# Differential attention's weights: Z0 moved out of the split, low halves subtracted on GpSimd, and four maxima sent through DRAM

## Chip, core and metric

One core of a Trainium2 chip runs the whole program. The metric is the device time of one execution in microseconds (us). TensorE (PE in the rows) does the matrix products, VectorE (DVE), ScalarE (ACT) and GpSimd (POOL) work on tiles of 128 partitions, and SyncE (SP) issues every DMA. Each engine works through its own list of instructions in order and waits at an instruction until what it needs is there.

## The reference, cut to what matters

One encoder layer for two groups of requests with the same weights: `p` (2048 positions) and `s` (512). An input projection gives eight units of heads: four for dilated window attention (mixer A, units 0 to 3) and four for differential attention (mixer B, units 4 to 7). This change is in mixer B:

```python
def diff_attention(q, k, v, lam, g_sub, lam_init):
    def block(qblk):                                   # 128 queries
        sc = jnp.einsum('bqhmd,bkhmd->bhmqk', qblk, k).astype(jnp.float32) * scale
        p = jax.nn.softmax(sc, axis=-1)
        a = p[:, :, 0] - lam * p[:, :, 1]
        return jnp.einsum('bhqk,bkhe->bqhe', a.astype(v.dtype), v)
    ...
    return rmsnorm(o, g_sub) * (1.0 - lam_init)
```

So two softmax maps over all keys are subtracted, the difference multiplies V, and each row of the product is divided by its root mean square. A factor common to a row of `a` cancels in that norm, but for the epsilon. The mixers' outputs then go through one output projection, a second norm and a gated residual.

## The kernel before

All inputs are float32. Each matrix product is made of float16 pairs: a value is scaled by a power of two, rounded to float16 (the high half), and the rest is rounded again (the low half); three products, high by high, high by low and low by high, are added. The scale of a weight block comes from its largest magnitude, which `allmax` finds over all partitions: TensorE transposes the column of 128 maxima (L178), VectorE takes the maximum of the row (L180), and a second matmul spreads it (L182).

The program goes through the units in the order 4, 0, 5, 1, 6, 2, 7, 3, so stages of mixer B and of mixer A alternate, B first. In each stage it goes through five blocks of 512 positions, four of `p` and one of `s`. While a unit's attention runs, the projections of its next block and of the next unit are woven in (`interleave`, with costs that set the pace), so that TensorE has work between the pieces of attention. The weight block two units ahead is loaded, scaled (`raw_scale`) and split (`raw_split`) in the same stages. A scheduler then lays down each engine's list from the order in which the code is written, priorities, and a timeline that it simulates.

A block of mixer B has four items of 128 queries (`ItemB`), 16 in `p` and 4 in `s` for each of the four units. For an item of `p`, per softmax map m (0 and 1) and half of the keys: TensorE makes 128 by 1024 scores in PSUM (L602, L608); VectorE scales them and keeps the row's minimum of the negated scores (L611); ScalarE takes the exponential into a tile of the pool `pp` and sums it into Z (L618). Then VectorE forms `a = p1 * (-lam * Z0 / Z1) + p0` (L634, two halves), ScalarE writes the high half, `a` times `rz[:, 3:4]`, that is sigc / Z0 (L636), VectorE the low half (L644, in `tail1`), and each of these is transposed by a DMA into `at`, two per item of high halves and two of low. An item later, `tail2` has TensorE multiply the transposed weights by V (L656, 48 matmuls into one PSUM tile of the pool `pv`), ScalarE squares and sums the result (L663) and copies it (L664), GpSimd works out the norm's factor in three small steps (L666, L668, L669). `tail3` scales the rows (ScalarE, L675), transposes them on TensorE (L677, again a tile of `pv`), and VectorE multiplies by the gate (L681). An item of `s` has one half of 512 keys for each map. In the stages of mixer B, `pv` has a single buffer: the product of one item, its transposition and the next item's product follow each other through it. The scores have three buffers (`sc`).

GpSimd also does the rotary embedding of Q and K (L443 to L446), whose results ScalarE copies on (L547, L488). `y_out` writes a finished block of 512 positions to DRAM and keeps its maximum; when all eight units have written a block, the output projection (`out_proj`, L918) can take it, after `y_scale` has worked out its scale.

## Time and profile before

| | us |
|---|---|
| median of 3 runs (2176.42 to 2187.44) | 2182.41 |
| the profiled execution's own time | 2191.28 |
| its span, first to last instruction | 2189.5 |
| TensorE busy | 1910.8 |
| VectorE busy | 1541.1 |
| ScalarE busy | 1152.7 |
| GpSimd busy | 394.9 |

The profiled execution took 8.9 us more than the median of the runs. Its granted TensorE clock is 0.942 of full speed on average. Busy time is an average over unlike stages, so it is read by stage below; TensorE's busy time counts matmuls that overlap, so a busy TensorE is not yet one at its peak.

### The profile page before, as it was taken

Reading aid. Unit: us, or ns where it says so; the run is one execution under the profiler, and the core shown is the slowest. Engines: PE = TensorE matmul, PEld = TensorE weight load, DVE = VectorE, ACT = ScalarE, POOL = GpSimd, SP = SyncE. Lnnn points to the kernel's source line nnn. Section 1 sums busy time; section 2 is a strip of 40 time slices with the busy share of each in tenths; the row PEclk is TensorE's granted clock in tenths of the full one; section 3 lists DMA queues with packets and bytes.
Section 4 is the critical chain, followed back from the end, with each engine's and each line's share of the span. In section 5 each row is a group of like instructions: output and inputs, shape, how many; then the busy total and the mean of one; then the engine's idle time right before and its main releaser. Section 6 shows DMA issues by size and latency. Waiting matters only on the chain. (4 is left out here: it accounts for less than half of the span.)

```text
span 2189.5 us, 47689 instructions
## 1 busy us (share of the span) xinstructions
PE 1910.8 (87%) x18545; PEld 1285.2 (59%) x18545; DVE 1541.1 (70%) x3428; ACT 1152.7 (53%) x2278; POOL 394.9 (18%) x1049
## 2 busy tenths in 40 slices
PE   4878997898989988888899888897989878989898
PEld 2665665666767666666566666574665554444443
DVE  3777998676669988666599886666888665455543
ACT  3555665555547666555467665554566644333321
POOL 0122222221112222111122221111222121100000
PEclk7789999999999999999999999898999888999999
DMA  7585787888857789898477888888776779665553
GB/s 293 171 253 126 138 163 149 188 158 165 186 130 152 145 196 188 140 173 192 114 151 145 184 188 155 170 183 235 147 148 157 159 163 191 122 133 126 130 163 111
DMA packets 726834, 360.12 MB, mean 164 GB/s; under 512 B 639808, under 2 KB 686672, under 8 KB 723152
## 3 DMA queue, kind: packets, MB, share of 16 engines
q1 hardware_dynamic: 726608, 357.08, 73.6%
q8 instruction: 145, 2.38, 0.5%
q14 instruction: 81, 0.66, 0.1%
HBM read 164.79 MB, written 36.97 MB: 92 GB/s over the span
## 5 line engine op out<-in xcount | busy, mean ns | idle before, releaser
L460 PE MATMUL pj<-w,h 128*128 128x256 f16 x3840 | 480.9, 281 | 29.1 <-DVE V L476 8.2
L460 PEld LDWEIGHTS <-h 128*128 128x128 f16 x3840 | 379.1, 101 | 103.9 <-issue 40.5
L618 ACT ACTIVATE pp<-sc,nb 128x1024 f32<-128x1024 f32 (+1 forms) x288 | 304.3, 1060 | 100.2 <-DVE sc L611 83.2
L534 PE MATMUL pj<-w,h 128*128 128x128 f16 x3840 | 257.1, 223 | 15.0 <-ACT q L541 8.5
L534 PEld LDWEIGHTS <-h 128*128 128x128 f16 x3840 | 231.6, 100 | 43.4 <-issue 32.5
L557 PE MATMUL pj<-h,w 128*128 128x512 f16 x960 | 230.7, 392 | 17.9 <-ACT q L541 17.9
L656 PE MATMUL pv<-V,at 128*128 128x128 f16 x3072 | 207.5, 227 | 38.1 <-DVE yt L681 29.0
L656 PEld LDWEIGHTS <-at 128*128 128x128 f16 x3264 | 201.9, 102 | 64.6 <-issue 47.8
L747 DVE SCALAR_TENSOR_TENSOR hl<-pp,Z,hl 128x640 f16<-128x640 f32 (+2 forms) x160 | 140.3, 881 | 119.4 <-DMA at<-hl 71.6
L443 POOL TENSOR_TENSOR rp<-q,tab_sb 128x64 f32<-128x64 f32 x160 | 67.3, 420 | 788.4 <-ACT q L466 469.5
L745 ACT ACTIVATE hl<-pp,Z 128x640 f16<-128x640 f32 (+2 forms) x160 | 130.3, 823 | 132.5 <-DMA at<-hl 108.7
L611 DVE TENSOR_SCALAR_CACHE_REDUCE sc<-sc,us,nb 128x1024 f32<-128x1024 f32 x128 | 172.3, 1346 | 37.1 <-PE sc L608 15.9
L611 DVE TENSOR_SCALAR_CACHE_REDUCE sc<-sc,us 128x1024 f32<-128x1024 f32 (+1 forms) x160 | 188.1, 1179 | 10.8 <-PE sc L608 10.2
L636 ACT ACTIVATE hl<-pp,rz 128x1024 f16<-128x1024 f32 (+1 forms) x144 | 155.6, 1095 | 60.7 <-issue 38.7
L731 ACT ACTIVATE pp<-pp,nb 128x640 f32<-128x640 f32 (+2 forms) x160 | 131.5, 822 | 105.9 <-DVE nb L726 100.1
L644 DVE SCALAR_TENSOR_TENSOR hl<-pp,rz,hl 128x1024 f16<-128x1024 f32 (+1 forms) x144 | 174.5, 1223 | 16.8 <-DMA at<-hl 5.9
L602 PE MATMUL sc<-K,Qc 128*128 128x512 f16 x512 | 158.6, 389 | 30.2 <-ACT pp L618 29.5
L557 PEld LDWEIGHTS <-w 128*128 128x128 f16 x960 | 94.1, 100 | 135.6 <-issue 42.0
L634 DVE SCALAR_TENSOR_TENSOR pp<-pp,rz,pp 128x1024 f32<-128x1024 f32 (+1 forms) x144 | 171.2, 1225 | 1.9
L918 PEld LDWEIGHTS <-w 128*128 128x128 f16 x960 | 92.9, 99 | 125.0 <-issue 17.0
L711 PE MATMUL sc<-K,Qc 128*32 128x512 f16 (+1 forms) x1024 | 119.2, 371 | 27.0 <-DMA Qc<-tq 17.1
L724 DVE CUSTOM_DVE_ANT_0 pp<-sc,maskp,us 128x384 f32<-128x384 f32 (+1 forms) x128 | 85.8, 678 | 71.0 <-PE sc L717 70.8
(200 smaller groups left out, 2843.9 us busy)
## 6 DMA issues: line engine op xcount, KB each, us to landing
h<-hp SPq DMA_DIRECT2D x124, 512.0 KB, 6.0
pp<-in_x_p_dram SPq DMA_DIRECT2D x32, 512.0 KB, 5.0
raw<-in_w_in_dram SPq DMA_DIRECT2D x8, 2048.0 KB, 8.1
h<-hs SPq DMA_DIRECT2D x32, 512.0 KB, 5.7
out_dram<-pp SPq DMA_DIRECT2D x20, 512.0 KB, 2.9
at<-hl SPq DMA_TRANSPOSE x608, 3.2
hp<-h SPq DMA_DIRECT2D x4, 2048.0 KB, 9.3
yp<-yt SPq DMA_DIRECT2D x32, 256.0 KB, 3.2
```

The source lines that it names most:

```text
L460: mm(ps[:, jj, :], lhsT=hT[:, a, k, j * P:(j + 1) * P], rhs=w[:, k, b, :], start=(k == 0 and i == 0), stop=(k == KT - 1 and i == 2))
L534: mm(ps[:, jj, 0:128], lhsT=hT[:, a, k, j * P:(j + 1) * P], rhs=w[:, k, b, 0:128], start=(k == 0 and i == 0), stop=(k == KT - 1 and i == 2))
L557: mm(ps, lhsT=w[:, k, b, 128:256], rhs=hT[:, a, k, :], start=(k == 0 and i == 0), stop=(k == KT - 1 and i == 2))
L602: mm(ps[:, n * 512:(n + 1) * 512], lhsT=Qc[:, j, m, 0, :], rhs=K[:, t:t + 4, m, :], start=True, stop=False)
L611: V.tensor_scalar(ps[:, :HW], ps[:, :HW], u["nsc"], nb[:, 0:1] if hf else 3e38, op0=ALU.mult, op1=ALU.min, accum_out=nb[:, hf:hf + 1])
L618: act(pt[m, hf][:, :HW], pss[hf][:, :HW], AF.Exp, scale=-1.0, bias=nb[:, NH - 1:NH], accum_out=Z[:, 2 * m + hf:2 * m + hf + 1])
L634: V.scalar_tensor_tensor(a, a, rz[:, 2:3], pt[0, hf][:, :HW], op0=ALU.mult, op1=ALU.add)
L636: act(hi[:, :HW], a, AF.Copy, scale=rz[:, 3:4])
L644: V.scalar_tensor_tensor(lo[:, :HW], a, sg, hi, op0=ALU.mult, op1=ALU.subtract)
L656: mm(po[:, :128], lhsT=a[:, k, :], rhs=Vv[:, k, 128 * b:128 * b + 128], start=(k == 0 and i == 0), stop=(k == NT - 1 and i == 2))
L731: act(sb[:, :NA], sb[:, :NA], AF.Exp, scale=-1.0, bias=nb[:, 1:2], accum_out=Z[:, 0:1])
L747: V.scalar_tensor_tensor(lo[:, :NA], sb[:, :NA], rz, hi[:, :NA], op0=ALU.mult, op1=ALU.subtract)
```

## The change

It has five parts. Line numbers in the diff's rows of the changed kernel differ from those of the kernel before by 12 to 24.

1. Z0 leaves the split. ScalarE's copy to the high half has no factor any more, and the low half is `a` minus its high half. For the range of float16 the first map's exponentials get a constant factor by way of their bias (`lnS`, made once with a logarithm; `nbs`, one small ScalarE addition per item). 1/Z0 comes back as a factor of the norm: GpSimd makes two small values from it per item instead of one.
2. The low halves are subtracted on GpSimd (`tail1`).
3. The four items' rows of a block are gathered in one tile (`st["o"]`), transposed by four matmuls into one PSUM tile, and multiplied by the gate in one instruction of 512 columns instead of four of 128.
4. `allmax_slow` takes the place of `allmax` in all but the first weight scale, the scale of the output weights, and the scales of `y`: the column of maxima goes to DRAM and comes back as a row on all partitions.
5. `y_scale` is called as soon as a block is complete (`y_out`) and no longer by the output projection's first tile.

```diff
-    sigc = C([P, 1], F32, "sigc")
-    V.reciprocal(sigc, lp1)
-    smul(sigc, sigc, 2.0 ** 13)
+    lnS = C([P, 1], F32, "lnS")
+    V.tensor_scalar_add(lnS, lp1, -1.0)
+    act(lnS, lnS, AF.Ln, scale=float(SMAX), bias=1.0)
+    V.tensor_scalar(lnS, lnS, -1.0, 14.0 * LN2, op0=ALU.mult, op1=ALU.add)
...
+    def allmax_slow(col):
+        d = dr.tile([P, 1], F32, tag=nm("amd"), name=nm("amd"))
+        nc.sync.dma_start(d, col)
+        row = T(tn, [P, P], F32, "amr", bufs=2)
+        nc.sync.dma_start(row, d.rearrange("p o -> (p o)").partition_broadcast(P))
+        m = T(tn, [P, 1], F32, "amc", bufs=2)
+        V.reduce_max(m, row, axis=AX.X)
+        return m
...
-        pow2(E, S, allmax(ag), f"w{g}")
+        pow2(E, S, (allmax if n == 0 else allmax_slow)(ag), f"w{g}")
...
+        if y_made[r, c] == NU:
+            y_scale(r, c)
...
+                nbs = T(tn, [P, 1], F32, "nbs")
+                if m == 0:
+                    act(nbs, nb[:, NH - 1:NH], AF.Identity, bias=lnS)
+                else:
+                    nbs = nb[:, NH - 1:NH]
...
-                    act(pt[m, hf][:, :HW], pss[hf][:, :HW], AF.Exp, scale=-1.0, bias=nb[:, NH - 1:NH],
+                    act(pt[m, hf][:, :HW], pss[hf][:, :HW], AF.Exp, scale=-1.0, bias=nbs,
...
-            V.tensor_scalar(rz[:, 2:3], zs[:, 0:1], rz[:, 1:2], nlam, op0=ALU.mult, op1=ALU.mult)
-            nc.gpsimd.tensor_tensor(rz[:, 3:4], rz[:, 0:1], sigc, op=ALU.mult)
+            V.tensor_scalar(rz[:, 1:2], zs[:, 0:1], rz[:, 1:2], nlam, op0=ALU.mult, op1=ALU.mult)
+            nc.gpsimd.tensor_scalar(rz[:, 2:3], rz[:, 0:1], rz[:, 0:1], u["k2"], op0=ALU.mult, op1=ALU.mult)
+            nc.gpsimd.tensor_tensor(rz[:, 3:4], rz[:, 0:1], u["kb"], op=ALU.mult)
...
-                act(hi[:, :HW], a, AF.Copy, scale=rz[:, 3:4])
+                act(hi[:, :HW], a, AF.Copy)
...
-                V.scalar_tensor_tensor(lo[:, :HW], a, sg, hi, op0=ALU.mult, op1=ALU.subtract)
+                nc.gpsimd.tensor_tensor(lo[:, :HW], a, hi, op=ALU.subtract)
...
-            self.o = T(ev, [P, P], F32, "o")
+            if j == 0:
+                st["o"] = T(ev, [P, 4, P], F32, "o", bufs=1)
+            self.o = st["o"][:, j, :]
...
-            pt_ = PT([P, 512], "pv")
-            nc.tensor.transpose(pt_[:, :128], self.o, id_sb)
-            yield 0.1
-            if "yt" not in st:
-                st["yt"] = T(qp, [P, 4, P], F32, "yt")
-            V.scalar_tensor_tensor(st["yt"][:, j, :], pt_[:, :128], gsub_sb, u["sg", c][:, j * P:(j + 1) * P],
-                                   op0=ALU.mult, op1=ALU.mult)
             if j == 3:
-                y_out(r, g, c, st["yt"].rearrange("p a b -> p (a b)"))
+                pt_ = PT([P, 4, P], "pv")
+                for q in range(4):
+                    nc.tensor.transpose(pt_[:, q, :], st["o"][:, q, :], id_sb)
+                yield 0.4
+                yt = T(qp, [P, 512], F32, "yt")
+                V.scalar_tensor_tensor(yt, pt_.rearrange("p a b -> p (a b)"), gsub_sb, u["sg", c],
+                                       op0=ALU.mult, op1=ALU.mult)
+                y_out(r, g, c, yt)
...
-        pow2(E, wo["S"], allmax(ag), "wo")
+        pow2(E, wo["S"], allmax_slow(ag), "wo")
...
-        pow2(s[:, 0:1], s[:, 1:2], allmax(ag), "y")
+        pow2(s[:, 0:1], s[:, 1:2], allmax_slow(ag), "y")
...
-        if j == 0:
-            y_scale(r, c)
```

What this makes of the engines' lists is seen at three places. First GpSimd in the second stage of mixer B (unit 5), before: rotary steps (L443 to L446), the factor of an item's norm (L666, L668, L669) and the item's sigc / Z0 (L629).

```order
L666 TENSOR_SCALAR rv_1422_9370<-ss_1421_9367,us_1223_7972 128x1
L668 TENSOR_TENSOR ro_1423_9372<-rv_1422_9370,mhalf_109 128x1
L669 TENSOR_TENSOR ro_1423_9372<-ro_1423_9372,us_1223_7972 128x1
L443 TENSOR_TENSOR rp1_1479_9689<-q32_1478_9687,tab_sb_103 128x64
L444 TENSOR_TENSOR rp2_1480_9690<-q32_1478_9687,tab_sb_103 128x4x8
L445 TENSOR_TENSOR rp2_1480_9690<-q32_1478_9687,tab_sb_103 128x4x8
L446 TENSOR_TENSOR q32_1478_9687<-rp1_1479_9689,rp2_1480_9690 128x4x16
L629 TENSOR_TENSOR rz_1434_9419<-rz_1434_9419,sigc_139 128x1
L666 TENSOR_SCALAR rv_1451_9542<-ss_1450_9539,us_1223_7972 128x1
```

The same engine in the same stage of the changed kernel (L455 to L458 are the rotary steps, L649 and L650 the two values from 1/Z0, L666 the low halves, L690, L692 and L693 the norm's factor).

```order
L649 TENSOR_SCALAR rz_1383_8996<-rz_1383_8996,us_1236_8008 128x1
L650 TENSOR_TENSOR rz_1383_8996<-rz_1383_8996,us_1236_8008 128x1
L666 TENSOR_TENSOR hl_1402_9105<-pp_1381_8991,hl_1385_9004 128x1024
L690 TENSOR_SCALAR rv_1400_9100<-ss_1399_9097,rz_1357_8828 128x1
L666 TENSOR_TENSOR hl_1403_9108<-pp_1382_8993,hl_1386_9008 128x1024
L692 TENSOR_TENSOR ro_1401_9102<-rv_1400_9100,mhalf_109 128x1
L455 TENSOR_TENSOR rp1_1424_9288<-q32_1423_9284,tab_sb_103 128x64
L456 TENSOR_TENSOR rp2_1425_9289<-q32_1423_9284,tab_sb_103 128x4x8
L457 TENSOR_TENSOR rp2_1425_9289<-q32_1423_9284,tab_sb_103 128x4x8
L693 TENSOR_TENSOR ro_1401_9102<-ro_1401_9102,rz_1357_8828 128x1
L458 TENSOR_TENSOR q32_1423_9284<-rp1_1424_9288,rp2_1425_9289 128x4x16
```

Two instructions of 1024 columns now stand behind each item's two small values, and the norm's factor of another item, and rotary steps, stand between or behind them.

Second TensorE in the same stage, before: the transposition of one item's rows (L677) between pieces of projections (L534, L557).

```order
L534 LDWEIGHTS h_1297_8579
L534 MATMUL pj_1447_9467<-w_794_4764,h_1297_8579 128x128
L677 MATMUL pv_1433_9416<-id_sb_97,o_1419_9365 128x128
L557 LDWEIGHTS w_794_4764
L557 MATMUL pj_1482_9700<-h_1297_8579,w_794_4764 128x512
```

TensorE in the same stage of the changed kernel (L622 are scores, L703 the transpositions, L569 a projection).

```order
L622 LDWEIGHTS Qc_1431_9313
L622 MATMUL sc_1606_10400<-K_906_5405,Qc_1431_9313 128x512
L703 MATMUL pv_1611_10430<-id_sb_97,o_1504_9769 128x128 x3
L569 LDWEIGHTS w_806_4794
L569 MATMUL pj_1627_10528<-h_1427_9300,w_806_4794 128x512
```

Three of a block's four transpositions stand together, the fourth 24 matmuls of a projection later, once per block; before there was one per item.

Third SyncE's list in the changed kernel, at the round trip of one weight block's maximum (`amd` is the column in DRAM, `amr` the row that comes back; L659 and L667 are transpositions of high and low halves, L383 a load of activations).

```order
L190 DMA amd_1017_6258<-ag_1014_6254 128x1
L383 DMA h_798_4767<-hp1_112 128x2048 x3
L659 DMA_TRANSPOSE at_87<-hl_731_4340 128x8x128
L506 DMA vbs0_124<-Vs_311_1790 128x2x256
L383 DMA h_798_4767<-hp1_112 128x2048
L503 DMA_TRANSPOSE Ks_310_1787<-tk_797_4761 128x2x128
L659 DMA_TRANSPOSE at_87<-hl_732_4344 128x8x128
L667 DMA_TRANSPOSE at_87<-hl_749_4451 128x8x128
L667 DMA_TRANSPOSE at_87<-hl_750_4454 128x8x128
L503 DMA_TRANSPOSE Ks_310_1787<-tk_797_4761 128x2x128
L192 DMA amr_1018_6260<-amd_1017_6258 128x128
```

Before, this list held neither of the two; the way back now stands behind two low halves' transpositions.

## Rows read from the trace of the kernel before

**Rows 1.** The page's first part: busy time, share and instructions of each engine.
```profile
PE 1910.8 (87%) x18545; PEld 1285.2 (59%) x18545; DVE 1541.1 (70%) x3428; ACT 1152.7 (53%) x2278; POOL 394.9 (18%) x1049
```

**Rows 2.** Windows by stage: length, PE, PEld, DVE, ACT, POOL busy, clock, DMA share, GB/s.
```profile
160.00:425.00 265.00, 232.41 (x2203) 161.76 (x2204) 216.80 (x375) 156.87 (x316) 63.82 (x161) 0.95 0.72 152
425.00:630.00 205.00, 178.23 (x2149) 136.37 (x2147) 126.14 (x387) 102.37 (x205) 29.36 (x93) 0.94 0.82 164
630.00:860.00 230.00, 211.75 (x2097) 146.04 (x2097) 206.70 (x352) 149.12 (x292) 56.73 (x143) 0.98 0.78 163
1065.00:1300.00 235.00, 216.97 (x2130) 148.82 (x2128) 205.75 (x351) 149.51 (x292) 57.20 (x142) 0.98 0.76 161
1505.00:1770.00 265.00, 227.11 (x2073) 151.15 (x2072) 209.83 (x352) 154.81 (x300) 54.54 (x136) 0.91 0.76 169
1770.00:2075.00 305.00, 274.28 (x2196) 141.77 (x2194) 166.80 (x451) 120.24 (x238) 30.03 (x76) 0.95 0.65 144
```

**Rows 3.** TensorE's waits in mixer B: total us, times, longest us.
```profile
PE pv L656 <- DVE yt L681: 32.9, 15, 4.6
...
PE sc L602 <- ACT pp L618: 31.8, 45, 3.4
...
PE pv L677 <- ACT o L675: 17.2, 14, 2.9
```

**Rows 4.** Groups of VectorE instructions: busy us, mean ns, idle time before.
```profile
L644 DVE SCALAR_TENSOR_TENSOR hl<-pp,rz,hl 128x1024 f16<-128x1024 f32 (+1 forms) x144 | 174.5, 1223 | 16.8 <-DMA at<-hl 5.9 <-ACT hl L636 5.7 <-issue 5.0
...
L681 DVE SCALAR_TENSOR_TENSOR yt<-pv,gsub_sb,sg 128x128 f32<-128x128 f32 x80 | 27.6, 344 | 9.4 <-PE pv L677 9.4
L562 DVE SCALAR_TENSOR_TENSOR sg<-sg,pj 128x512 f32<-128x512 f32 x40 | 27.3, 682 | 29.9 <-ACT sg L561 29.8
```

**Rows 5.** Groups, then single lines with shortest, median, longest ns: GpSimd and VectorE.
```profile
L443 POOL TENSOR_TENSOR rp<-q,tab_sb 128x64 f32<-128x64 f32 x160 | 67.3, 420 | 788.4 <-ACT q L466 469.5 <-ACT q L541 307.9 <-DVE Z L118 8.5
L444 POOL TENSOR_TENSOR rp<-q,tab_sb 128x32 f32<-128x32 f32 x160 | 51.1, 319 | 0.0
...
L443 POOL TENSOR_TENSOR rp<-q,tab_sb x160: 317/320/1647, 83.9 to 1968.4; 128x64 f32<-128x64 f32 x160
...
L444 POOL TENSOR_TENSOR rp<-q,tab_sb x160: 244/253/1237, 84.1 to 1968.6; 128x32 f32<-128x32 f32 x160
...
L634 DVE SCALAR_TENSOR_TENSOR pp<-pp,rz,pp x144: 736/1280/1444, 182.8 to 1785.2; 128x1024 f32<-128x1024 f32 x128, 128x512 f32<-128x512 f32 x16
```

**Rows 6.** ScalarE's waits for GpSimd: total us, times, longest us.
```profile
ACT o L675 <- POOL ro L669: 90.5, 49, 3.4
...
ACT tq L547 <- POOL q L446: 54.7, 48, 6.1
...
ACT tk L488 <- POOL q L446: 25.0, 18, 2.9
```

**Rows 7.** Timeline of an item in unit 5: start us, us, engine, line.
```profile
704.28 2.48 DVE L634 SCALAR_TENSOR_TENSOR pp<-pp,rz,pp 128x1024 f32<-128x1024 f32 x2
...
705.87 1.07 POOL L443 TENSOR_TENSOR rp<-q,tab_sb 128x64 f32<-128x64 f32 x1 [2.18 <-ACT q L466]
705.96 2.19 ACT L636 ACTIVATE hl<-pp,rz 128x1024 f16<-128x1024 f32 x2
...
709.48 2.48 DVE L644 SCALAR_TENSOR_TENSOR hl<-pp,rz,hl 128x1024 f16<-128x1024 f32 x2
```

**Rows 8.** Small DMAs from issue to landing (us, at the end), and the low halves' transpositions.
```profile
w<-gg SPq DMA_DIRECT2D x2, 512.0 KB, 5.5
...
gg<-hl SPq DMA_DIRECT2D x1, 8.0 KB, 1.3
...
DMA to landing us min/median/max: 2.4/3.3/9.3
```

**Rows 9.** ScalarE at the start: a table load, and a small activation with its wait.
```profile
0.71 1.28 ACT L194 ACT_TABLE_LOAD   x1 [0.71 <-PEq L1170]
...
10.33 0.20 ACT L153 ACTIVATE le<-ld 128x2 f32<-128x2 f32 x1 [7.23 <-DVE ld L150]
```

More of the change, by code (lines that the diff above doesn't have):

```diff
@@ L331, in unit_scalars @@
             kap = s[:, 4:5]
-            V.tensor_scalar(kap, lp1, iS, 2.0 ** 5, op0=ALU.mult, op1=ALU.mult)
+            smul(kap, iS, 2.0 ** 18)
             u["k2"] = s[:, 5:6]
@@ L627, in front @@
             V.reciprocal(rz[:, 0:2], zs)
-            V.tensor_scalar(rz[:, 2:3], zs[:, 0:1], rz[:, 1:2], nlam, op0=ALU.mult, op1=ALU.mult)
-            nc.gpsimd.tensor_tensor(rz[:, 3:4], rz[:, 0:1], sigc, op=ALU.mult)
+            V.tensor_scalar(rz[:, 1:2], zs[:, 0:1], rz[:, 1:2], nlam, op0=ALU.mult, op1=ALU.mult)
+            nc.gpsimd.tensor_scalar(rz[:, 2:3], rz[:, 0:1], rz[:, 0:1], u["k2"], op0=ALU.mult, op1=ALU.mult)
+            nc.gpsimd.tensor_tensor(rz[:, 3:4], rz[:, 0:1], u["kb"], op=ALU.mult)
+            self.rz = rz
             self.ah, self.al = at_pair(3, S // P, P)
@@ L633, in front @@
                 a = pt[1, hf][:, :HW]
-                V.scalar_tensor_tensor(a, a, rz[:, 2:3], pt[0, hf][:, :HW], op0=ALU.mult, op1=ALU.add)
+                V.scalar_tensor_tensor(a, a, rz[:, 1:2], pt[0, hf][:, :HW], op0=ALU.mult, op1=ALU.add)
                 hi = T(hl, [P, 1024], F16, "hl")
-                act(hi[:, :HW], a, AF.Copy, scale=rz[:, 3:4])
+                act(hi[:, :HW], a, AF.Copy)
                 nc.sync.dma_start_transpose(out=self.ah[:, hf * 8:hf * 8 + HW // P, :], in_=hi[:, :HW])
-                self.lo.append((a, hi[:, :HW], rz[:, 3:4]))
+                self.lo.append((a, hi[:, :HW]))
         def tail1(self):
             HW = min(1024, SQ[self.a[0]])
-            for hf, (a, hi, sg) in enumerate(self.lo):
+            for hf, (a, hi) in enumerate(self.lo):
                 lo = T(hl, [P, 1024], F16, "hl")
-                V.scalar_tensor_tensor(lo[:, :HW], a, sg, hi, op0=ALU.mult, op1=ALU.subtract)
+                nc.gpsimd.tensor_tensor(lo[:, :HW], a, hi, op=ALU.subtract)
                 nc.sync.dma_start_transpose(out=self.al[:, hf * 8:hf * 8 + HW // P, :], in_=lo[:, :HW])
@@ L665, in tail2 @@
             v = T(tn, [P, 1], F32, "rv")
-            nc.gpsimd.tensor_scalar(v, ss, u["k2"], EPS_T, op0=ALU.mult, op1=ALU.add)
+            nc.gpsimd.tensor_scalar(v, ss, self.rz[:, 2:3], EPS_T, op0=ALU.mult, op1=ALU.add)
             self.rst = T(tn, [P, 1], F32, "ro")
             nc.gpsimd.tensor_tensor(self.rst, v, mhalf, op=ALU.pow)
-            nc.gpsimd.tensor_tensor(self.rst, self.rst, u["kb"], op=ALU.mult)
+            nc.gpsimd.tensor_tensor(self.rst, self.rst, self.rz[:, 3:4], op=ALU.mult)
             yield 0.05
@@ L675, in tail3 @@
             act(self.o, self.o, AF.Copy, scale=self.rst)
-            pt_ = PT([P, 512], "pv")
-            nc.tensor.transpose(pt_[:, :128], self.o, id_sb)
-            yield 0.1
-            if "yt" not in st:
-                st["yt"] = T(qp, [P, 4, P], F32, "yt")
-            V.scalar_tensor_tensor(st["yt"][:, j, :], pt_[:, :128], gsub_sb, u["sg", c][:, j * P:(j + 1) * P],
-                                   op0=ALU.mult, op1=ALU.mult)
-            if j == 3:
-                y_out(r, g, c, st["yt"].rearrange("p a b -> p (a b)"))
+            if j == 3:
+                pt_ = PT([P, 4, P], "pv")
[6 more added lines that the diff above has]
+                y_out(r, g, c, yt)
+            yield 0.0
     def krange(r, c):
@@ L877, in y_scale @@
         V.reduce_max(ag, yam[:, c + (r == "s") * NSB["p"], :], axis=AX.X)
-        s = T(tn, [P, 4], F32, "ys")
-        pow2(s[:, 0:1], s[:, 1:2], allmax(ag), "y")
+        s = T(tn, [P, 4], F32, "ys", bufs=5)
+        pow2(s[:, 0:1], s[:, 1:2], allmax_slow(ag), "y")
         V.tensor_scalar(s[:, 0:1], s[:, 0:1], wo["i"], None, op0=ALU.mult)
```

## The prediction

> **What bounds the kernel now.** The page's totals come first: TensorE is busy 87% of the span, VectorE 70%, ScalarE 53%, GpSimd 18% [rows 1]. An average over unlike stages decides nothing, so the windows by stage come next [rows 2]. In the second and third stage of mixer B VectorE is busy 206.70 of 230 us and 205.75 of 235 (90% and 88%), in the first and last 82% and 79%; in the stage of mixer A shown it is at 62%. The part of the change that takes work off VectorE can therefore pay only in the four stages of mixer B, 265 + 230 + 235 + 265 = 995 us. TensorE is busy there 232.41 + 211.75 + 216.97 + 227.11 = 888.2 us, so it idles 106.8 us. That is the most that shorter waits can give back, but for the clock: its granted mean is 0.95, 0.98, 0.98 and 0.91 of full speed. Between its two levels, 1.2 and 2.4 GHz, such a mean says that twice the missing share ran at the lower one: 26.5 + 9.2 + 9.4 + 47.7 = 93 us, half of it lost, 46 us. The lowest mean stands in the stage where TensorE idles most, 38 us.
>
> Then TensorE's waits [rows 3]. 32.9 us go to the product with V waiting for VectorE's gate multiplication, 17.2 us to the transposition waiting for ScalarE's scaled rows (these two are the single buffer of `pv`), 31.8 us to scores waiting for an exponential to free their buffer. The last wait is VectorE's doing in part: the exponential stands behind the scaling of the scores, and that stands in one list with the combinations and low halves [rows 7].
>
> **Low halves on GpSimd.** Removed from VectorE: 144 instructions of 1223 ns on average, 174.5 us [rows 4], all but the few at a stage's end in mixer B; call it 167 us there. VectorE's load in the four stages falls from 216.8 + 206.7 + 205.8 + 209.8 = 839 us to some 672. No instruction of 1024 columns on GpSimd is in the trace. The nearest are rotary steps of 64 and 32 columns, with medians of 320 and 253 ns [rows 5]: 2.1 ns a column and 186 ns fixed, so 2.33 us for 1024 and 1.26 us for 512. Lower bound: VectorE's own 1.28 us for the like [rows 5, 7]. Upper bound: from the means, 420 and 319 ns, which hold waits: 3.2 ns a column, 3.5 us. I take 2.33, by the undisturbed medians: 128 x 2.33 + 16 x 1.26 = 318 us, on an engine that is busy 232 of the 995 us [rows 2]. The second small value per item adds 80 x 0.25 = 20 us, the 32-column step being the nearest row. GpSimd comes to 570 us, 57%; with 3.5 us to some 725, 73%. It has the time; what matters is who queues behind it.
>
> The Trainium skill, GPSIMD Engine Reference, section 3 (Performance versus the Vector engine), speaks against the move: elementwise work with two inputs belongs on VectorE, and GpSimd takes 4497 ns for a sum of 2048 columns where VectorE takes 2293. An estimate by its two-input cost of 2.6 cycles a column is 2.2 us for 1024, so the term would come to about 310 us and the sum would stay: the row's price already holds the slower rate.
>
> Is a low half later for it? In the timeline [rows 7] the first high half ends about 1.1 us into the pair that starts at 705.96, at 707.1; VectorE starts the first low half at 709.48, after scalings of scores, and ends the second at 711.96. GpSimd, through with its four rotary steps by about 707.8, would end the second at 707.8 + 2 x 2.33 = 712.5. So low halves come at nearly the same time: slower work, but not in VectorE's queue.
>
> **Rows gathered by four.** 80 gate multiplications of 344 ns become 20 of 512 columns, 682 ns by the nearest row [rows 4]: 27.6 - 13.6 = 14 us off VectorE. More important, three items in four pass through `pv` without a transposition, so three quarters of 32.9 + 17.2 us [rows 3] go: -38 us (bounds: 0, if another wait ends last in the same place, to -50). The fourth item's transposition now waits for a factor of the norm that can stand behind a low half on GpSimd, as the order shows. Twenty of these, each late by 0 to 2.33 us, cost 0 to 47 us; the order puts 24 matmuls of a projection between the third and the fourth transposition, so I take +8.
>
> **VectorE relieved.** The scores' wait, 31.8 us, loses half by choice: -16 (bounds 0 to -32). With waits nearly halved, a third of the clock's 46 us: -15 (0 to -46).
>
> **The small parts.** The round trip of a maximum costs a landing of 1.3 us for a small store and up to 5.5 us for the broadcast [rows 8], 6.8 us, against three short instructions before; there are 13 (seven weight blocks, the output weights, five blocks of y). The weights' scale is needed a stage later, and VectorE has 15 instructions between the column and the row's maximum at the place where the order shows SyncE. Cost 0 to 88 us, taken as +6: the cover is other VectorE work, and if it is gone, VectorE stands still and the scores behind it too. SyncE's wait for the column holds up the transpositions behind it, whose own landing is 3.3 us at the median [rows 8]. Calling `y_scale` early costs nothing: the projection that needs it comes later. The logarithm brings two table loads, 1.28 us each [rows 9]; the first falls into a wait of ScalarE for inputs, so +1.3 (0 to 2.6). The 80 additions `nbs`, 0.20 us each by the small activation there, are 16 us of ScalarE, which is busy 610 of 995 us; two other score buffers cover them, 0 (up to +16). High halves without a factor: 0, same instruction.
>
> **Sum.** -38 - 16 - 15 + 8 + 6 + 1 = -54 us against the execution's own 2191.3 (span 2189.5), 2137. That execution lies 8.9 us above the median; taken off the median, 2182.4 - 54 = **2128 us**. What a measurement of this kernel tells from no change is about 0.5%, 11 us.
>
> **Rivals.** *ScalarE behind GpSimd (slower).* ScalarE waits 90.5 + 54.7 + 25.0 = 170 us for GpSimd already, some 143 of it in mixer B if half of the middle one is [rows 6]. Its list has 160 such places there, by the code (80 scaled rows, 80 copies of Q and K). If each found one whole low half in front, 160 x 2.33 = 373 us more: ScalarE would need 610 + 143 + 16 + 373 = 1142 us in stages of 995, 147 more than there is, against 54 gained: about 2275. It decides when the extra wait passes (941 - 610 - 143 - 16) / 160 = 1.1 us a place, and is a loss for the whole from there on. With half of the places hit it is 2182 to 2220. For it: the order puts the norm's steps between two low halves. Against: other places have them in front, and the scheduler moves ScalarE's copies too. 0.20.
>
> *VectorE shut out by GpSimd.* Rotary steps of a median 320 ns take up to 1647 [rows 5], and one that begins at 705.87, while VectorE combines halves from two SBUF tiles, ends only when that pair does, near 706.8 [rows 7]: one waits for the other. VectorE's combinations are hardly longer for it, 1444 at most against 1280 [rows 5], but GpSimd's instructions were short. The Trainium skill, SBUF — State Buffer, section Who interferes with whom, has the rule: a VectorE instruction with two SBUF inputs and a GpSimd instruction that reads SBUF exclude each other for a whole instruction. The trace agrees for GpSimd's side. For this kernel: 256 VectorE instructions of that kind by the code (144 combinations, 80 residuals of Q and K, 32 weight splits), low halves running 318 of 941 us, 34%, half of 2.33 us left on average: 256 x 0.34 x 1.17 = 102 us. VectorE would be at 672 - 10 + 102 = 764 of 941, 81%, nearly as now; the relief goes, the gain in `pv` stays: -38 + 15 = -23, 2159 us. Still faster. 0.14.
>
> *Nothing changes.* TensorE is at 92% in the two inner stages [rows 2] and waits elsewhere by the order of its list; a low half that lands later stalls the product with V instead of `pv`, and 54 us come back as 16 us a stage: 2182, within 0.5%. 0.14.
>
> *More gained.* If all of VectorE's waits go, up to the bounds -50 - 32 - 46: 2060 to 2085. 0.10.
>
> **How the numbers follow.** The forecast, 2085 to 2170 with 2128 as its middle, holds 0.42. Faster by over 0.5%: 0.42 + 0.10 + 0.14 = 0.66; within 0.5%: 0.14; slower: 0.20. The range runs from 2070 to 2205 us: below it lie some 0.06 of the larger gain, above it 0.12 of the slower rival.
>
> **What would show it.** VectorE's share in the four stages falls from 79 to 90% to 65 to 75%, GpSimd's rises to 55 to 65%, and the stages shorten by 10 to 20 us each, the first and last most; the stages of mixer A keep their 205 us. The new GpSimd instruction has a median near 2.33 us, its longest a VectorE combination more. TensorE's wait for the gate multiplication falls below 12 us. The forecast is wrong if ScalarE's waits for GpSimd grow by more than 150 us, if VectorE's combinations stretch far beyond 1444 ns, if the product's wait for transposed low halves becomes TensorE's longest, or if VectorE waits for the returned row.

## The result, and the profile after

The changed kernel takes 2330.84 us (median of 4 runs, 2320.23 to 2338.53) against 2182.86 for the kernel before beside it: a ratio of 1.0677, 95% interval 1.0626 to 1.0728. It is slower by 148 us where 54 us of gain were forecast. The profiled execution has a span of 2327.2 us, 137.7 more than before.

The page's totals come first, in the form of [rows 1].

```profile
PE 1941.2 (83%) x18506; PEld 1300.9 (56%) x18506; DVE 1433.3 (62%) x3224; ACT 1159.6 (50%) x2361; POOL 689.3 (30%) x1273
```

VectorE has 108 us less to do, as was meant, and GpSimd 294 more. TensorE idles 107 us more, and is busy 30 us longer for nearly the same matmuls: its mean granted clock fell from 0.942 to 0.929. Estimated in the prediction's way, with twice the missing share at 1.2 instead of 2.4 GHz and half of that lost, the clock cost 0.071 x 2327 - 0.058 x 2190 = 38 us more than before. (The six kernels with round trips in this document have means of 0.927 to 0.937, the fourteen others 0.938 to 0.951.) Next the windows of the stages of [rows 2], at their new places, with the same columns.

```profile
164.00:435.00 271.00, 227.30 (x2203) 158.92 (x2204) 193.78 (x332) 159.68 (x338) 136.00 (x213) 0.96 0.71 151
435.00:641.00 206.00, 175.29 (x2151) 133.03 (x2150) 124.76 (x374) 100.65 (x202) 30.73 (x98) 0.94 0.81 161
641.00:905.00 264.00, 222.05 (x2166) 152.88 (x2165) 190.53 (x350) 158.79 (x335) 132.58 (x202) 0.96 0.70 146
1121.00:1398.00 277.00, 229.27 (x2143) 155.88 (x2141) 186.02 (x334) 154.86 (x327) 129.29 (x199) 0.93 0.68 138
1600.00:1890.00 290.00, 236.64 (x2197) 159.21 (x2195) 197.44 (x344) 163.99 (x339) 129.19 (x200) 0.93 0.74 162
1890.00:2205.00 315.00, 277.47 (x2058) 138.11 (x2058) 148.26 (x400) 110.38 (x209) 26.99 (x69) 0.92 0.59 132
```

By these windows the loss lies above all in mixer B's second and third stages, which were the densest: 230 us became 264, 235 became 277, and TensorE's idle time in them went from 18 to 42 and 48 us. The first stage of mixer A took 206, as before. How much falls to which stage depends on where the windows are cut: cut at mixer B's first and last score matmuls, its second and third stages took 20 and 32 us longer, the stage of mixer A between them 23. The waits say who is late now (engine, line and tile, what ended the wait: total us, times, longest). TensorE's:

```profile
PE pv L678 <- DMA at<-hl: 120.8, 66, 9.2
PE pv L790 <- DMA at<-hl: 45.3, 22, 8.7
PE sc L616 <- ACT pp L637: 23.4, 22, 4.0
PE pj L941 <- ACT w L917: 20.0, 1, 20.0
```

VectorE's two longest, and one of SyncE's:

```profile
DVE sc L625 <- PE sc L622: 142.8, 87, 7.3
DVE amc L194 <- DMA amr<-amd: 104.0, 13, 16.2
```
```profile
SPq L192 <- DMA amd<-ag: 62.1, 10, 9.0
```

Two of these waits as they were in the kernel before:

```profile
DVE sc L611 <- PE sc L608: 26.0, 21, 5.2
...
PE pv L656 <- DMA at<-hl: 9.0, 11, 2.2
```

Of the waits of [rows 3] for the gate multiplication and the scaled rows, 0.8 and 1.6 us are left. In their place the product (L678) waits 120.8 us for transposed weights, 9.0 before. Those who waited, asked by the line that issues the transpositions (high halves, L659, then low halves, L667):

```profile
L659 SPq DMA_TRANSPOSE at<-hl x144: 1188/1236/8360, 195.3 to 1896.7; - x144
...
  PE pv L678: 109.7, 54
```
```profile
L667 SPq DMA_TRANSPOSE at<-hl x144: 1188/1278/4102, 198.0 to 1898.1; - x144
...
  PE pv L678: 11.1, 12
```

So it is the high halves, which were not moved to GpSimd, that the product waits for. VectorE stands 104.0 us at the returned row of maxima, 8.0 us for each of 13 trips, and 142.8 us for scores (26.0 before): the time freed on it became waiting. The two transfers of a trip, from issue to landing (KB each, median us):

```profile
amr<-amd SPq DMA_DIRECT2D x13, 64.0 KB, 4.7
amd<-ag SPq DMA_DIRECT2D x13, 0.5 KB, 8.5
```

One trip in the third stage of mixer B, the one with the longest way back of the thirteen, on SyncE and on VectorE (start us, us, line; in brackets the idle time before):

```profile
1351.32 0.53 SPq L190 DMA_DIRECT2D amd<-ag  x1
...
1359.95 2.05 SPq L192 DMA_DIRECT2D amr<-amd  x1
1362.11 3.41 SPq L659 DMA_TRANSPOSE at<-hl  x1
```
```profile
1360.29 0.17 DVE L647 RECIPROCAL rz<-zs 128x2 f32<-128x2 f32 x1
1369.71 0.29 DVE L194 TENSOR_REDUCE amc<-amr 128x1 f32<-128x128 f32 x1 [9.26 <-DMA amr<-amd]
...
1370.22 2.48 DVE L656 SCALAR_TENSOR_TENSOR pp<-pp,rz,pp 128x1024 f32<-128x1024 f32 x2
```

The column leaves at 1351.32 and the row is there at 1369.71: 18.4 us. Until 1359.95 SyncE may not issue the way back, and the transposition of a high half stands behind it; from 1360.46 until 1369.71 VectorE does nothing, and the next item's combinations stand behind that. GpSimd's side, by contrast, went as forecast: a low half of 1024 columns took 2.13 us (estimated 2.33), and ScalarE's wait for the norm's factor even fell, from the 90.5 us of [rows 6] to 57.0.

```profile
L666 POOL TENSOR_TENSOR hl<-pp,hl x144: 1152/2127/2830, 195.3 to 1893.4; 128x1024 f16<-128x1024 f32 x128, 128x512 f16<-128x512 f32 x16
```
```profile
ACT tq L559 <- POOL q L458: 57.9, 45, 3.7
ACT o L699 <- POOL ro L693: 57.0, 49, 3.7
```

### The profile page after: what moved, and what is told of

Read it like the earlier page. It is cut to its first block, busy times and chain, and to the rows that moved or that the text cites. A ratio compares the mean times of both kernels' runs of the same rounds, so it can differ in the third digit from the quotient of the medians.

```text
span 2327.2 us, 47751 instructions
## 1 busy us (share of the span) xinstructions
PE 1941.2 (83%) x18506; PEld 1300.9 (56%) x18506; DVE 1433.3 (62%) x3224; ACT 1159.6 (50%) x2361; POOL 689.3 (30%) x1273
## 5 line engine op out<-in xcount | busy, mean ns | idle before, releaser
L666 POOL TENSOR_TENSOR hl<-pp,hl 128x1024 f16<-128x1024 f32 (+1 forms) x144 | 294.6, 2058 | 149.3 <-ACT hl L658 100.6
L678 PE MATMUL pv<-V,at 128*128 128x128 f16 x3072 | 230.2, 229 | 125.2 <-DMA at<-hl 115.7
L678 PEld LDWEIGHTS <-at 128*128 128x128 f16 x3264 | 205.9, 103 | 180.1 <-DMA at<-hl 145.5
L546 PE MATMUL pj<-w,h 128*128 128x128 f16 x3840 | 270.9, 225 | 22.0 <-DVE V L488 7.7
L455 POOL TENSOR_TENSOR rp<-q,tab_sb 128x64 f32<-128x64 f32 x160 | 63.2, 395 | 685.3 <-ACT q L478 435.0
L569 PE MATMUL pj<-h,w 128*128 128x512 f16 x960 | 223.6, 387 | 11.0 <-ACT q L553 11.0
L637 ACT ACTIVATE pp<-sc,nb 128x1024 f32<-128x1024 f32 (+1 forms) x144 | 152.3, 1062 | 95.3 <-DVE sc L625 92.1
L658 ACT ACTIVATE hl<-pp 128x1024 f16<-128x1024 f32 (+1 forms) x144 | 143.7, 1004 | 98.3 <-DVE pp L656 85.2
L616 PE MATMUL sc<-K,Qc 128*128 128x512 f16 x512 | 158.8, 390 | 24.6 <-ACT pp L637 23.4
L756 ACT ACTIVATE pp<-pp,nb 128x640 f32<-128x640 f32 (+2 forms) x160 | 131.3, 821 | 93.6 <-DVE nb L751 86.3
L569 PEld LDWEIGHTS <-w 128*128 128x128 f16 x960 | 93.4, 99 | 122.7 <-issue 26.0
L637 ACT ACTIVATE pp<-sc,nbs 128x1024 f32<-128x1024 f32 (+1 forms) x144 | 152.3, 1061 | 13.7 <-DVE masks L361 7.2
L941 PE MATMUL pj<-raw,w 128*128 128x512 f16 x480 | 122.9, 390 | 20.4 <-ACT w L917 20.0
```

The source lines that it names most:

```text
L546: mm(ps[:, jj, 0:128], lhsT=hT[:, a, k, j * P:(j + 1) * P], rhs=w[:, k, b, 0:128], start=(k == 0 and i == 0), stop=(k == KT - 1 and i == 2))
L569: mm(ps, lhsT=w[:, k, b, 128:256], rhs=hT[:, a, k, :], start=(k == 0 and i == 0), stop=(k == KT - 1 and i == 2))
L616: mm(ps[:, n * 512:(n + 1) * 512], lhsT=Qc[:, j, m, 0, :], rhs=K[:, t:t + 4, m, :], start=True, stop=False)
L637: act(pt[m, hf][:, :HW], pss[hf][:, :HW], AF.Exp, scale=-1.0, bias=nbs, accum_out=Z[:, 2 * m + hf:2 * m + hf + 1])
L658: act(hi[:, :HW], a, AF.Copy)
L666: nc.gpsimd.tensor_tensor(lo[:, :HW], a, hi, op=ALU.subtract)
```

## The experiments

Theories at the start: the round trips of the maxima are the loss; or the low halves on GpSimd are; or the order of the lists, which puts the product with V too early once the rows are gathered. Times are medians, the kernel before run beside them (2181 to 2184 us in each set).

### Round trips and low halves undone, one at a time and together

Maxima on TensorE (first run; the output weights and `y` likewise), low halves on VectorE (second), both (third); the edits, cut:

```diff
-        pow2(E, S, (allmax if n == 0 else allmax_slow)(ag), f"w{g}")
+        pow2(E, S, allmax(ag), f"w{g}")
...
-                nc.gpsimd.tensor_tensor(lo[:, :HW], a, hi, op=ALU.subtract)
+                V.tensor_tensor(lo[:, :HW], a, hi, op=ALU.subtract)
```

> The changed kernel with every maximum over partitions taken on TensorE again, as before the change; all else as changed. Three theories. Round trip: VectorE's 104 us of waiting for the returned row, and SyncE's 62 us of waiting for the column with the transpositions queued behind it, are the loss; then most of the 148 us between the kernels goes, 2190 to 2240 us. Low halves: their place on GpSimd is the loss; then the round trips were mostly hidden and this run stays at 2300 or above. Order: the rows gathered by four and the changed stages of an item let the scheduler put the product with V too early, so that TensorE waits 120 us for transposed high halves; then this run stays at 2270 or above, and that wait above 100 us.

> The changed kernel with the low halves subtracted on VectorE again (still without a factor); all else as changed, the round trips too. Round trip: VectorE gets some 167 us of work more and keeps waiting for the returned row: 2320 to 2400 us, no better than the changed kernel. Low halves: the loss goes, 2200 to 2250. Order: 2290 to 2360, with TensorE's wait for transposed high halves still above 100 us.

> The changed kernel with both undone: maxima on TensorE and low halves on VectorE; what is left of the change is the rows gathered by four, the weights not divided by Z0 with the norm's new factors, and the early scale of y. Round trip and low halves together explain everything: 2160 to 2190 us, since by the prediction's own sum the gathering is worth up to 38. Order: 2250 or above.

The fourth puts the round trips alone into the kernel before.

> The kernel before with only the round trips of maxima put in (weights but the first, output weights, blocks of y, whose scale is still taken late). Round trip: 13 trips at about 8.5 us for the store and 4.7 us for the row, VectorE standing still for most of each and the transpositions queued behind SyncE's wait: 2250 to 2330 us. Order or low halves: 2180 to 2220.

| kernel | us | ratio to before (interval) |
|---|---|---|
| maxima on TensorE | 2249.24 | 1.0302 (1.0267 to 1.0338) |
| low halves on VectorE | 2323.49 | 1.0647 (1.0616 to 1.0679) |
| both | 2225.48 | 1.0208 (1.0173 to 1.0244) |
| before, with round trips | 2271.76 | 1.0408 (1.0381 to 1.0436) |

The first run lies between the ranges of its theories, with the product still waiting 112.5 us for transposed halves; the third lies in neither of its two ranges. Three pairs differ in the round trips alone: 2330.84 - 2249.24 = 82 us, 2323.49 - 2225.48 = 98, and 2271.76 - 2183.83 = 88. Each is more than half of the loss of 148 us. In the fourth kernel VectorE and SyncE wait as in the changed one:

```profile
DVE amc L192 <- DMA amr<-amd: 110.9, 13, 13.5
```
```profile
SPq L190 <- DMA amd<-ag: 72.1, 12, 7.9
```

The low halves on GpSimd cost 24 us without round trips (2249.24 - 2225.48) and 7 with them: not the main loss, but no gain either. And with both undone 42 us remain.

### What remains: gathering, Z0, the early scale of y

The kernel with both undone was run with one transposition per item again, and with `y_scale` late again; the kernel before with the gathering alone; and the kernel before with only Z0 moved and the low halves on GpSimd.

> The kernel with both undone (maxima on TensorE, low halves on VectorE), and the rows gathered by four undone as well: one transposition and one gate multiplication per item. What is left is the weights not divided by Z0 and the early scale of y. It stands at 2225 us with the gathering. Gathering is the rest of the loss: 2175 to 2195 us, and TensorE's wait for transposed high halves falls from 177 to below 60 us. Weights not divided by Z0 (their high half no longer waits for GpSimd in the scheduler's order, so the product is put early): 2215 to 2245 us, with that wait still near 150.

> The kernel before with only the rows gathered by four. The prediction's price for this part was -38 + 8, so 2150 us. If gathering is what remains of the loss after maxima and low halves: 2210 to 2235. If it is the weights not divided by Z0: 2150 to 2185.

> The kernel with both undone (2225 us), and the scale of y taken late again, where the projection needs it. If the early call puts short VectorE work and two transpositions for the maximum into the stages: 2205 us or less, most of it from the ends of the stages of mixer A. If it costs nothing, as the prediction had it: 2218 to 2235.

> The kernel before with the weights not divided by Z0 and the low halves on GpSimd, and nothing else of the change: no gathering, maxima on TensorE, the scale of y late. Prediction's price for this part: -16 - 15, so 2150 us. If low halves on GpSimd cost what they do beside the gathering (2249 against 2225 us): 2190 to 2215. If VectorE's relief pays only without the gathering: below 2175.

Measured: 2207.74 (ratio 1.0128, 1.0091 to 1.0166), 2209.08 (1.0121, 1.0080 to 1.0161), 2232.84 (1.0242, 1.0210 to 1.0274) and 2229.19 us (1.0224, 1.0179 to 1.0270). The first lies between its two ranges, the fourth above all of its own. The kernel with the gathering alone takes 28 us more, the one with Z0 moved (and the early scale of `y`) 26. The early scale costs nothing that is seen: late again the kernel was 7 us slower. No part is seen to gain. Two of TensorE's waits in the kernel before with the gathering:

```profile
PE pv L656 <- DMA at<-hl: 72.9, 51, 4.5
...
PE pv L656 <- DVE yt L684: 2.9, 6, 1.0
```

The gathering does what the prediction said, the wait for the gate multiplication is down from 32.9 us to 2.9, and the product then waits 72.9 us for weights instead of 9.0. With low halves on GpSimd, and nothing gathered, VectorE is busy 1433 us instead of the 1538 of the kernel with Z0 moved alone, and its longest wait is for TensorE (44.0 us there):

```profile
DVE sc L623 <- PE sc L620: 96.4, 55, 5.9
```

### Is it the place of the product, and what in a round trip costs?

The gathering kernel with the product's chunks in falling order, so that it begins with the half transposed last (cut; the marks for the first and last chunk follow):

```diff
-                for k in range(NT):
+                for k in range(NT - 1, -1, -1):
```

> The kernel before with the rows gathered by four (2209 us), and the product with V taking its 16 chunks of keys in falling order, so that its first matmul needs the high half that is transposed last. List order: the gathering cost time because the product, no longer held back by its single buffer, was put where the first high half arrives; now it can't be put there, TensorE's wait for transposed high halves falls from 73 to below 35 us, and the time to 2165 to 2190. If the gathering costs time by something else (the fourth item's four transpositions, the buffer of four rows): 2200 us or more.

2212.63 us (1.0129, 1.0099 to 1.0160), the wait 56.4 us. A miss: the wait shrank by 16.5 us, not to below 35, and the time did not fall. So it isn't shown that this wait is what the gathering costs.

The kernel before with the trips, both ways, issued from GpSimd's queue; with the trips made on SyncE and the row never read (maxima on TensorE); and with the trips on GpSimd's queue, never read (cut, against the kernel before with round trips):

```diff
-        nc.sync.dma_start(d, col)
+        nc.gpsimd.dma_start(d, col)
...
-        m = T(tn, [P, 1], F32, "amc", bufs=2)
-        V.reduce_max(m, row, axis=AX.X)
-        return m
+        return allmax(col)
```

> The kernel before with the round trips (2272 us), both of their transfers issued from GpSimd's queue instead of SyncE's. If the loss is SyncE standing at its wait for the column with the high halves' transpositions behind it: 2200 us or less. If it is VectorE standing still until the row comes back: 2245 to 2290, with VectorE's wait for the row still near 110 us or above.

> The kernel before with the round trips' transfers on SyncE as changed, but nobody reads the returned row: the maximum is taken on TensorE as before. If VectorE standing still until the row comes back is the loss: 2180 to 2200 us. If it is SyncE's wait and the transfers themselves: 2240 or above.

> The kernel before with the round trips' transfers made but never read, as in the run that took 2236 us, now issued from GpSimd's queue instead of SyncE's. If SyncE's 83 us at the wait between the two transfers, with high-half transpositions behind it, are the 54 us that this run lost: 2180 to 2200 us. If it is the transfers on the DMA engines, or only that the list is another: 2220 to 2245.

Measured: 2259.84 (1.0361, 1.0327 to 1.0395), 2236.01 (1.0257, 1.0221 to 1.0293) and 2248.69 us (1.0299, 1.0268 to 1.0330). The second and third lie just outside the ranges for SyncE's wait and the transfers, the first inside that for VectorE, though its wait for the row fell to 67.6 us. Unread trips still cost 54 and 66 us. Reading the row adds 2271.76 - 2236.01 = 36 us on SyncE's queue, 11 on GpSimd's; these two differences lie within what another order of the lists costs (below), so the share of VectorE's standing still is not known.

The 54 us of the first unread kernel are another matter, because no other order stands behind them. The traces of it and of the kernel before hold the same instructions of VectorE, ScalarE and GpSimd in the same order, by source line and tile, and TensorE's differ at 29 places of 18545. What differs is SyncE's list, with 26 transfers more and four moved. Between the two transfers of a trip SyncE now stands:

```profile
SPq L190 <- DMA amd<-ag: 83.1, 12, 9.5
```

Compared matmul by matmul, the profiled execution falls 44 us behind that of the kernel before. It falls back by 4.2 to 9.5 us within 25 us of the store in nine of the thirteen trips, by -2.7 to 1.0 in the other four. That is 49 us in all; elsewhere it makes up a few. One of the nine, on SyncE and TensorE, then the same place before (L756 and L748 transpose high halves of mixer A):

```profile
608.10 0.52 SPq L188 DMA_DIRECT2D amd<-ag  x1
608.73 1.46 SPq L581 DMA_DIRECT2D yp<-yt  x1
615.98 0.33 SPq L190 DMA_DIRECT2D amr<-amd  x1
616.42 1.19 SPq L756 DMA_TRANSPOSE at<-hl  x1
```
```profile
621.29 0.27 PE L773 MATMUL pv<-at,Vs 128*128 128x128 f16 x1 [5.72 <-DMA at<-hl]
```
```profile
605.79 0.53 SPq L573 DMA_DIRECT2D yp<-yt  x1
607.07 1.18 SPq L748 DMA_TRANSPOSE at<-hl  x1
```

The transposition follows the store of `y` after 7.7 us instead of 1.3, and TensorE stands 5.7 us for a transposed half, where before it did not wait. In six of the nine trips TensorE waits for transposed halves, 24 us in all and none at the same matmuls before; in the other three it waits longer than before for activations or for an operand of the output projection, which also come over SyncE's queue. Over the whole kernel the two mixers' products wait 54 us for transposed halves, 21 before (9.0 us for mixer B's, above, and the last row here for mixer A's):

```profile
PE pv L773 <- DMA at<-hl: 32.9, 19, 5.7
...
PE pv L664 <- DMA at<-hl: 21.4, 13, 4.6
```
```profile
PE pv L765 <- DMA at<-hl: 12.3, 12, 3.8
```

So the unread trips cost in the main by what they hold up on SyncE's queue; whether their transfers also slow others on the DMA engines is not shown. The kernel with them on GpSimd's queue does not speak against this, nor for it: there GpSimd's own list stands 113.1 us at the same wait, and the lists of all engines are laid down otherwise. From mixer B's last score matmul to the end the six kernels with trips, read or not, take 437 to 443 us, the fourteen without them 413 to 429; in the first unread kernel, five of whose trips lie there, it is 439 against 415, 24 of the 44 us.

### Z0 without the small additions

The kernel with round trips, low halves and gathering undone, its constant factor on the high halves, and likewise on the low ones, instead of in the exponentials' bias (cut):

```diff
-                    act(nbs, nb[:, NH - 1:NH], AF.Identity, bias=lnS)
...
-                act(hi[:, :HW], a, AF.Copy)
+                act(hi[:, :HW], a, AF.Copy, scale=sigc)
```

> The kernel with maxima on TensorE, low halves on VectorE and no gathering (2208 us: what is left is the weights not divided by Z0, and the early scale of y), but with the constant factor applied to the high and low halves, as a constant column, instead of to the exponentials' bias: the 80 small additions on ScalarE between a maximum and its exponentials go, all else stays. If those additions are the loss, 26 us: 2178 to 2192. If it is the high half that no longer waits for GpSimd's product, or the norm's second factor on GpSimd, or the early scale: 2200 to 2215.

2206.00 us (1.0098, 1.0064 to 1.0133) against 2207.74: without the 80 additions the kernel is no faster, so no loss from them is seen.

### What does another order cost by itself?

Three kernels that change no instruction's work, only how the lists fall. The first hands over after every eighth chunk, the second exchanges the two ScalarE instructions that read a product, the third (0.27 in place of 0.23) announces another cost. Then the first two again with the gathering.

```diff
-                    if k % 4 == 3:
-                        yield 0.23
+                    if k % 8 == 7:
+                        yield 0.46
...
-            act(jk, po[:, :128], AF.Square, accum_out=ss)
             act(self.o, po[:, :128], AF.Copy)
+            act(jk, po[:, :128], AF.Square, accum_out=ss)
```

> The kernel before with no instruction added, removed or changed: the product with V hands over after every eighth chunk, with twice the cost, instead of after every fourth. Only the lists' order changes. If small losses (26 to 28 us for the gathering, for the weights not divided by Z0) are what any other order of these lists costs: 2195 to 2215. If those parts cost by what they themselves do: 2175 to 2190.

> The kernel before with the two copies of a product on ScalarE (its squares, its rows) made in the other order, nothing else. If any other order of the lists costs some 25 us: 2195 to 2215. If the parts cost by what they do: 2175 to 2190.

> The kernel before with the cost that the product with V announces for four chunks set to 0.27 instead of 0.23, so that the merging of the pieces falls otherwise; no instruction changes. If any other order of the lists costs some 25 us: 2195 to 2215. If the parts cost by what they do: 2175 to 2190.

> The kernel before with the rows gathered by four, and the product handing over after every eighth chunk: the same change of order alone that brought the kernel before from 2182 to 2196 us. If the gathering costs by what it does, this stands some 27 us above that, 2215 to 2230. If its 27 us were one draw of the order, it may fall anywhere from 2175 to 2235, and below 2200 would show it.

> The kernel before with the rows gathered by four, and the two copies of a product on ScalarE made in the other order, which alone brought the kernel before from 2182 to 2189 us. If the gathering costs by what it does: 2208 to 2225. If it was one draw of the order: anywhere from 2175 to 2235, and below 2195 would show it.

| order | before, us | with gathering, us | wait of product for weights, us |
|---|---|---|---|
| as written | 2181.44 | 2209.08 (1.0121) | 9.0 and 72.9 |
| every eighth chunk | 2195.54 (1.0052, 1.0030 to 1.0075) | 2227.11 (1.0212, 1.0170 to 1.0255) | 24.7 and 67.2 |
| copies exchanged | 2188.92 (1.0023, 1.0004 to 1.0041) | 2211.23 (1.0120, 1.0089 to 1.0152) | 16.1 and 84.3 |
| announced cost 0.27 | 2234.15 (1.0229, 1.0195 to 1.0263) | | 30.3 |

Order alone moved the kernel before by 7, 13 and 52 us, always up; the 52 were in neither range. So a single difference of 25 us between two kernels whose lists differ says nothing of the part that was changed. The gathering, though, costs 28, 32 and 22 us in three orders, and 18 with Z0 moved (2225.48 - 2207.74), the first three each time with the same wait in its place. The wait does not set the price: the kernel with the longest, 84.3 us, lost least of the three, and the kernel before with the announced cost lost 52 us at 30.3. Two rows of TensorE's waits show it, from the gathering kernel and the kernel before, both with the copies exchanged:

```profile
PE pv L656 <- DMA at<-hl: 84.3, 59, 6.7
```
```profile
PE pv L656 <- DMA at<-hl: 16.1, 18, 2.2
```

The lists agree: TensorE's holds the 48 matmuls of a product in one piece 27 to 37 times in the four orders without gathering, and 8 to 13 times with it, where it puts the first 8, those of the first half's columns, by themselves 64 to 75 times.

## Why the prediction was wrong, point by point

**Round trips, "taken as +6": the step that failed most.** They cost 82 to 98 us in three pairs, about the upper bound of 88 that stood beside it. Three things were wrong. A trip was priced at 6.8 us from a store of 8 KB (1.3 us) and a broadcast of 512 KB; the store of 128 single values took 8.5 us at the median and 13.6 at most, the way back 4.7. The cover, VectorE's instructions between the two, was counted in the list; in the trip shown they lasted until 1360.46 and the row came 9.3 us later. And the wait that weighs most as far as the pairs show, SyncE's for the column, was named ("holds up the transpositions behind it") and got no price of its own: with nobody reading the row, and the other engines' lists as before, 54 us are lost, at the trips, where TensorE waits for what stands behind SyncE's wait. The case in which "the cover is gone" was written down too, with "VectorE stands still and the scores behind it too", and it got no chance. What VectorE's standing still adds is not known: 36 and 11 us in two pairs, each with other lists. The Trainium skill, DMA: Bandwidth & Descriptors, section Anatomy of one DMA, puts the fixed cost of a transfer on GpSimd's path near 2 us; here the store of 512 B took 9.6 us at the median on GpSimd's path (7.3 to 11.5, the kernel that reads the row) and 8.5 on SyncE's, far above it, and the measurement decides. Its section Specifications says that pieces under 512 B don't move at line rate, which these of 4 B would fit; no run here varies their size.

**Gathering, -38 and +8: wrong in sign.** The waits named went away, as said. The bound "0, if another wait ends last in the same place" was too kind: without the single buffer of `pv` to hold it back, the product's first chunks stand by themselves in the list, and it waits longer, for the high halves, than it had waited for the gate multiplication. It is 22 to 32 us slower in three orders out of three. That this wait is the price is argued, not shown: with falling chunks it was 16.5 us shorter and the time no less, and why stays open.

**VectorE relieved, -16 and -15.** VectorE lost 108 us of work, and the scores' wait for an exponential fell from 31.8 to 23.4 us, half of what was taken. But the clock went the other way, 0.942 to 0.929, with TensorE idle 107 us more. (That fall goes with the round trips: with low halves on GpSimd and neither trips nor gathering the mean is 0.941, 0.943 with Z0 moved alone.) Low halves on GpSimd cost 24 and 7 us in the two clean pairs, and 21 in a third that also differs in when `y` is scaled; all are within what another order costs. So the gain of 31 us was not seen in any pair, and why they lose is not shown. VectorE was 90 and 88% busy in two stages, but taking work off it did not shorten the chain: relieved, it waited for scores, 142.8 us instead of 26.0, and 96.4 without trips and gathering.

**GpSimd's price, 2.33 us, ScalarE behind it, small parts.** The price was right (2.13), and so was the low chance for ScalarE behind GpSimd. The rule of the Trainium skill cited against the move (GPSIMD Engine Reference, section 3) held: GpSimd took 2.13 us for a width that costs VectorE 1.28. Z0 moved, at nothing: it measured 26 us with the early scale of `y`, 24 with a constant factor, within the range of order alone, so its own cost is not known. The additions took 0.29 us each, not 0.20, and leaving them out gained nothing. Three sums are slightly off and decide nothing: 128 x 2.2 + 16 x 1.1 is some 300, not 310; in the second rival the gathering should take 14 us off VectorE, not 10; and 54 us over four stages are 13.5 each, not 16.

**VectorE shut out by GpSimd.** It is seen, and small. VectorE's subtraction of Q's residual, shortest, median and longest ns, with low halves on VectorE and on GpSimd (the kernels with maxima on TensorE):

```profile
L560 DVE TENSOR_TENSOR tq<-q,tq x80: 399/420/427, 88.2 to 1998.9; 128x256 f16<-128x256 f32 x80
```
```profile
L560 DVE TENSOR_TENSOR tq<-q,tq x80: 403/424/1934, 90.0 to 2028.4; 128x256 f16<-128x256 f32 x80
```

In the second kernel six of the 80 took over 1.5 us. They are the six that began while GpSimd was in a low half, and each ended within 0.3 us of that low half's end: one waits for the other, but the two seldom meet. In the changed kernel the group takes 43.5 us against 33.6; the combinations, one of which took 3147 ns, together only some 3 us more than before. The 102 us of that rival, worked out as if a third of 256 instructions met a low half, were far too many.

**Nothing changes, as a rival,** named the right place: a later half stalls the product instead of `pv`. It named the low half; it was the high one. Of the four signs listed as refuting the forecast, VectorE waits for the returned row, and the product's wait for transposed halves is TensorE's longest, though for the other halves; ScalarE's waits for GpSimd did not grow, and VectorE's combinations stayed short but for one. VectorE's share in the four stages, 67 to 72%, is as forecast, GpSimd's, 45 to 50%, below the 55 to 65%: neither decided anything.

The terms, as measured: round trips 88, gathering 28, Z0 with the early scale 26, low halves 24, together 166 against 148. They add up only roughly, as parts that each carry a draw of the order must. Shown is the sign of the trips and of the gathering, and of the trips' 88 us how 54 come about; what Z0 and the low halves cost by themselves stays open.

## What to carry to other kernels

Price a round trip through DRAM by its two landings, from a transfer of the same shape, and by what stands behind the wait between them on the issuing queue; count the cover in microseconds, not in instructions. A wait that ends last hides the next one: before a buffer's wait is booked as a gain, ask which transfer the freed instruction will stand at, and read that transfer's landing. Where a scheduler lays down the lists, run two or three orders of the unchanged kernel first: here they spread over 52 us, and a part worth less than that needs several orders to be seen, or a pair whose lists are the same: then the place where one falls behind the other can be read off, as at the unread trips.

## What the hardware showed unexpectedly

A store of 512 B, 4 B from each of 128 partitions, landed after 7.2 to 13.6 us (median 8.5), mostly longer than the 64 KB that came back from it (3.1 to 9.7, median 4.7); on GpSimd's queue it was no quicker (7.3 to 11.5). GpSimd subtracted 1024 columns in 2.13 us, and single VectorE instructions that began in such a subtraction took 1.9 and 3.1 us instead of 0.42 and 1.28, but rarely.
